# A modulation sum copied a step later, two more steps before transposing o, and a last tail of four slots

## The chip, the cores and the metric

The kernel runs on one core of a Trainium2 chip. The metric is device time in microseconds, the median of the runs of one program. All times inside the kernel are from one profiled execution and are counted from the start of its span.

## What is computed

Two transformer blocks on a sequence of 256 tokens of width 1024, in float32. The first has a SwiGLU feed-forward, a mixing layer of retention and neighbourhood attention, and a second SwiGLU. The second block has two layers, each an attention (the first blockwise, the second differential) and a squared-ReLU feed-forward, both followed by a layer norm with a gated residual. Shift, scale and gate of each come from sums over a second input `c`:

```python
mod = jnp.einsum('bd,lde->lbe', jax.nn.silu(c), ada_w) + ada_b[:, None, :]
for i in range(DEPTH_2):
    shift1, scale1, gate1, shift2, scale2, gate2 = [m[:, None, :] for m in jnp.split(mod[i], 6, axis=-1)]
    h = x * (1.0 + scale1) + shift1
    y = moba_attention(h, ...) if i % N_MIXERS == 0 else diff_attention(h, ...)
    x = layer_norm(DEEPNORM_ALPHA * x + (1.0 + gate1) * y, ln_g[i, 0], ln_b[i, 0])
    h = x * (1.0 + scale2) + shift2
    y = sq_relu_mlp(h, mlp_w_up[i], mlp_w_down[i])
    x = layer_norm(DEEPNORM_ALPHA * x + (1.0 + gate2) * y, ln_g[i, 1], ln_b[i, 1])
```

In the differential attention, with 8 heads of 128 columns:

```python
p = jax.nn.softmax(s, axis=-1)
w = (p[:, :, 0] - lam * p[:, :, 1]).astype(v.dtype)
o = jnp.einsum('bhqk,bhke->bhqe', w, v)
o = rms_norm(o, subln_g) * (1.0 - lambda_init)      # then @ w_out
```

## The kernel before

**Weights.** All weights stream through a ring. A slot is 1 MB of weights and has two halves, called pieces, of 128 x 1024 each. `load` (L70) brings a piece into one of 6 raw buffers, on SP's queue. `piece` (L103) makes two parts of it: ScalarE copies it, rounded, to `wh` (L115), and VectorE subtracts that from the raw one to make `wl` (L93), one piece behind (`flush`). A ring of 8 pieces holds them. Each product is three matmuls (L201): high by high, low by high, high by low. A half slot is 12 matmuls of 512 columns or 24 of 256, about 2.7 us.

**Steps.** The kernel is one sequence of instructions, written out in the order in which it is issued, and each engine takes its own in that order. After every half slot `tick` (L430) runs: `st.tick` issues up to two pieces ahead, or one piece of a modulation sum, and then `bg` (L415) advances every generator in `gens` by one step. A `yield n` in a generator waits n steps. `start(gen, wait)` (L424) lets a generator begin `wait` steps after the `bg` that comes next. What is issued in a step stands, on each engine, behind all that was issued before it and ahead of the matmuls of the next half slot. An instruction that waits holds up its engine.

**Modulation sums.** Twelve sums, one for each of six vectors in two layers. Each has 8 pieces of `ada_w`; VectorE adds each, multiplied by a column of silu(c), to `adacc` (L339). After the last, `ada_parts` (L346) splits the sum into three bfloat16 parts, one instruction a step: ScalarE's copy (L349), a subtraction (L351), a second copy (L353), a second subtraction (L355). The first piece of the next sum drains what is left (`ada_drain`, L403). A finished sum waits in `ada_out`, and `spare` (L373), called when a hidden tile has been made, issues 24 small matmuls that reduce it over the partitions (or, for a gate, spread it).

**Second attention** (`attention(1, ...)`, L1219). Slots: 2 for v of heads 0 to 3, then q and k of each two heads, then v of heads 4 to 7, then the output projection. `pair(j, q, k)` (L1234) is the generator of head j: scores and row maxima, a step, exponentials, a step, VectorE combines the two softmaxes (L1271), one or two steps, transposition of the scores and ScalarE's copy T (L1280, L1281), a step, the product with v (tile `ao`, L1302), ScalarE's squares (L1312), POOL's power, a step, VectorE scales o (L1318), and, for heads below `ONE[1][1]`, a step; then TensorE transposes o (L1322), and ScalarE and VectorE make the high and low parts of Y (L1328, L1329), which the output projection reads. `down` (L510) multiplies a slot into four PSUM banks, half by half. `down_tail` (L520) does the last two slots bank by bank, so that a bank's post-processing (`post.bank`) begins while the next bank is multiplied.

**Last feed-forward** (`mlp`, L750). For j from 2 to 15, `proj` multiplies up-slot j and starts `hidden(j)` (ScalarE's ReLU L778, VectorE's product L779, a step, high and low parts L546, L547), and `down` follows three tiles behind. After the loop come `down` of tile 13, then `down_tail` of tiles 14 and 15. Four tiles are kept. The last post-processing (`Last`, L672) makes for each bank a product with the gate, the residual, statistics (L650 to L652), and, for two banks that share rows, the mean and variance, POOL's power, four passes of normalisation (L681, L683) and the stores (L684).

Of the kernel before, what the change touches and what calls it, by code (L numbers as in the profile page):

```python
# [37 lines left out]
       ((2, 0), (1, 0), (1, 1), (1, 2), (1, 3), (0, 2), (0, 3)))  # L38
LOOK = 3.0
WAITS = ((0, 1, 0, 1, 0, 1, 0, 1), (0, 1, 0, 1, 0, 1, 0, 1))  # L40
ONE = ((7, 8), (8, 6))
RET_WAITS = (1, 3, 1, 3)
NA_WAITS = (3, 2, 5, 4)

# [127 lines left out]
def block_kernel(ctx, tc, A, out):  # L172
# [157 lines left out]
    def ada(key, h, w):  # L330
        l, s, i = key
        kb = 2 * i + h
        if kb == 0:
            ada_drain()
            adacc[0] = big.tile([128, D], F32, name="adacc")
            V.tensor_scalar(adacc[0], w, csil[:, 0:1], None, op0=OP.mult)
            return
        t = adacc[0]
        V.scalar_tensor_tensor(t, w, csil[:, kb:kb + 1], t, op0=OP.mult, op1=OP.add)  # L339
        if kb == 7:  # L340
            ada_now.append(ada_parts(l, s, t))
            start(ada_now[0])

    ada_now, ada_done = [], {}

# [14 lines left out]
    ada_out, adap, grows = [], [], {}  # L360
# [50 lines left out]
    def nxt():  # L411
        wi_[0] += 1
        return wi_[0] - 1
# [10 lines left out]
    def start(gen, wait=0):  # L424
        gens.append([gen, wait + 1])
# [15 lines left out]
    def mmA(o, wh, wl, x, s, e):  # L441

        mm(o, x[:, 0], wh, s, False)
        mm(o, x[:, 0], wl, False, False)
        mm(o, x[:, 1], wh, False, e)

    TS = (slice(0, 128), slice(128, 256))
# [62 lines left out]
    def down(accs, H, first):  # L510
        n = nxt()
        for kk, (wh, wl) in enumerate(st.use(n, D)):
            for t in range(2):
                for f in range(2):
                    fs = slice(512 * f, 512 * f + 512)
                    mmA(accs[t][f], wh[:, 0, fs], wl[:, 0, fs], H[:, kk, :, TS[t]], first and kk == 0, False)
            st.release(n, kk)
            tick()

    def down_tail(accs, hs, post, mid):  # L520

        ns = [nxt(), nxt()]
        w = [st.use(n, D) for n in ns]
        for t in range(2):
            for f in range(2):
                fs = slice(512 * f, 512 * f + 512)
                for i in range(2):
                    for kk in range(2):
                        wh, wl = w[i][kk]
                        mmA(accs[t][f], wh[:, 0, fs], wl[:, 0, fs], hs[i][:, kk, :, TS[t]], False, i == 1 and kk == 1)  # L530
                    if t and f and i == 0:
                        mid()
                if t and f:
                    for n in ns:
                        for h in range(2):
                            st.release(n, h)
                if t and f:
                    post.bank(t, f, st.ahead)
                    st.flush(post.low)
                else:  # L540
                    post.bank(t, f)
                    tick()
# [205 lines left out]
        down_tail(accs, [hid.pop(n - 2), hid.pop(n - 1)], p, mid)  # L748

    @with_exitstack  # L750
    def mlp(cx, turn, after, post, mid):
        hp = cx.enter_context(tc.tile_pool(name="hid", bufs=1))
        n = DFF2 // 256
        hid = {}
        accs = None

        def tile_of(j):
            hid[j] = hp.tile([128, 2, 2, S], F32R, name="H", bufs=4)
            return hid[j][:, :, 0], hid[j][:, :, 1]

        def hidden01(ps):
            q = [w2("q"), w2("q")]
            for t in range(2):
                SC.activation(q[t], ps[t], AF.Relu)
                V.tensor_tensor(q[t], q[t], ps[t], OP.mult)
            yield 1
            for j in range(2):
                for c in range(2):
                    for t in range(2):
                        PE.transpose(two(ps[j])[:, c, TS[t]], q[t][:, (2 * j + c) * 128:(2 * j + c + 1) * 128], ident)  # L770
                split(*tile_of(j), two(ps[j]))
            if ada_out:
                yield 1
                yield from spare(ps[0])

        def hidden(j, p):
            q = w2("q")
            SC.activation(q, p, AF.Relu)  # L778
            V.tensor_tensor(q, q, p, OP.mult)  # L779
            yield 1  # L780
            split(*tile_of(j), two(q))
            yield from spare(p)

        ps = [gu("u"), gu("u")]
        projT(ps, turn, lambda: start_now(hidden01(ps)))
        after()
        for j in range(2, n):
            b = gu("u")
            proj(b, lambda: start_now(hidden(j, b)))
            if j >= 3:  # L790
                if accs is None:
                    accs = [[acc("acc") for _ in range(2)] for _ in range(2)]
                down(accs, hid.pop(j - 3), j == 3)
        down(accs, hid.pop(n - 3), False)
        while n - 1 not in hid:
            bg()
        mid[0]()
        p = post(accs)
        down_tail(accs, [hid.pop(n - 2), hid.pop(n - 1)], p, lambda: mid[1](p))
        return p  # L800

    lam = const.tile([128, 2], F32, name="lam")
# [384 lines left out]
    mid, first = ffn_block(G_F2PRE)  # L1187
# [31 lines left out]
    def attention(l, turn, after, mid):  # L1219
        with tc.tile_pool(name=f"att{l}", bufs=1) as mp:  # L1220
# [13 lines left out]
            def pair(j, q, k):  # L1234
# [7 lines left out]
                hs = [slice(0, 64), slice(64, 128)]  # L1242
# [34 lines left out]
                for a in range(nh):  # L1277
                    p = acc("at")
# [6 lines left out]
                if tail:  # L1285
                    yield from room(1)
                    p = acc("ao")
                    live[0] += 1
                    late = 1
                else:  # L1290
                    p = gu("ao")
# [25 lines left out]
                    for c in range(2):  # L1317
                        V.tensor_scalar(two(o)[:, c], two(p)[:, c, 0:128], r[:, c:c + 1], None, op0=OP.mult)  # L1318
                if j < ONE[l][1]:
                    yield 1  # L1320
                for c in range(2):
                    PE.transpose(two(p)[:, c, 128:256], two(o)[:, c], ident)  # L1322
                yh, yl, p = two(YH[:, j]), two(YL[:, j]), two(p)[:, :, 128:256]
# [15 lines left out]
            vdone, tail = set(), []  # L1339
# [34 lines left out]
            accs = [[gu("oacc") for _ in range(2)] for _ in range(2)]  # L1374
# [4 lines left out]
            post = PostLn(accs, grows.pop((l, 2)))  # L1379
# [21 lines left out]
    def after_ln(l, i):  # L1401

        ac = []

        def prep():
            g, b = ln_cols(l, i)
            ln, s = (l, 3) if i == 0 else (l + 1, 0)
            ac.extend(ln_mod(f"m{l}{i}", g, b, plus1(f"s{l}{i}", modc(ln, s + 1)), modc(ln, s)))

        def mid(post):  # L1410
            turns[0] = turn_of(post.v, *ac, gu if i else acc)
            turns[0](0)
        return prep, mid

    post = None
    for l in range(2):
        last, ln = post, ln_rows(0, 1) if l else None
        post = attention(l, only1(turns[0]), (lambda: start(last.residual(ln), 1)) if l else nothing, after_ln(l, 0))
        with ada_pool():
            last, ln = post, ln_rows(l, 0)  # L1420
            post = mlp(only1(turns[0]), lambda: start(last.residual(ln), 1),
                       (lambda accs: Last(accs, grows.pop((1, 5)), ln_rows(1, 1))) if l else
                       lambda accs: PostLn(accs, grows.pop((0, 5))), (nothing, nothing) if l else after_ln(0, 1))


_SHAPES = {"x": (256, 1024), "ffn1_w_in": (1024, 5632), "ffn1_w_out": (2816, 1024), "w_mix_in": (1024, 6656),
# [61 lines left out]
```

## Time and profile before

| | us |
|---|---|
| median of 3 runs | 1298.73 (1296.03 to 1302.18) |
| the profiled execution | 1299.73 |
| its span, first to last instruction | 1297.8 |
| TensorE busy | 1244.4 |
| VectorE busy | 930.2 |
| ScalarE busy | 644.9 |
| mean granted clock of TensorE | 0.982 |

PE is TensorE, PEld its weight loads, DVE VectorE, ACT ScalarE, SP the engine that issues loads. The granted clock is a share of 2.4 GHz. A matmul's row shows when it began and a modelled end, so a stream of matmuls is best read by their starts.

### The profile page before, as it was taken

To read this page: it belongs to the slowest core of one execution; us is meant where nothing else is said; L and a number is where in the kernel's file an instruction comes from. 1 tells how busy PE (TensorE), PEld (TensorE's weight loads), DVE (VectorE), ACT (ScalarE), POOL (GpSimd) and SP (SyncE) were. 2 spreads that over 40 slices of the span, in tenths; PEclk is the share of its full clock that TensorE was granted. 3 is DMA by queue.
4 is the path that set the end of the run, shared out by engine and by line. 5 is a ranking of instruction groups with operands and counts; after the bars stand their busy time and mean duration, and the time that the engine had idled before them with its cause. 6 is when DMAs were issued, how large, how long until landed. Compare 5 with 4: busy or idle time off the path is not lost. (4 is left out here: it accounts for less than half of the span.)

```text
span 1297.8 us, 18953 instructions
## 1 busy us (share of the span) xinstructions
PE 1244.4 (96%) x7216; PEld 1071.9 (83%) x7222; DVE 930.2 (72%) x1292; ACT 644.9 (50%) x1040; POOL 37.9 (3%) x45
## 2 busy tenths in 40 slices
PE   8999989999999999999999999999989889999996
PEld 7888767888988878888889978999968877799995
DVE  5687757888677676868478657777877966775655
ACT  6453445655555465354456545544544455544440
POOL 0000000220000000000000000000000001000000
PEclk9999989999999999999999999999998999999998
DMA  8778676766556477988454346788865434576650
GB/s 299 265 257 288 220 254 176 249 206 199 211 186 224 158 236 239 313 277 285 157 179 134 110 130 197 250 282 277 273 208 168 131 98 146 168 246 220 225 195 33
DMA packets 167883, 271.67 MB, mean 209 GB/s; under 512 B 15888, under 2 KB 119664, under 8 KB 167792
## 3 DMA queue, kind: packets, MB, share of 16 engines
q1 hardware_dynamic: 161328, 268.36, 63.0%
q10 hardware_dynamic: 6464, 2.10, 0.7%
q8 instruction: 57, 0.93, 0.3%
q14 instruction: 34, 0.28, 0.1%
HBM read 269.37 MB, written 1.05 MB: 208 GB/s over the span
## 5 line engine op out<-in xcount | busy, mean ns | idle before, releaser
L93 DVE TENSOR_TENSOR wl<-raw,wh 128x1024 fp32r<-128x1024 f32 x392 | 467.8, 1220 | 48.9 <-ACT wh L115 48.1
L115 ACT ACTIVATE wh<-raw 128x1024 fp32r<-128x1024 f32 x392 | 398.0, 1054 | 143.1 <-issue 21.5
L201 PE MATMUL acc<-wh,H 128*128 128x512 f32 x864 | 283.4, 396 | 3.0 <-ACT wh L115 3.0
L201 PE MATMUL g<-wh,XX 128*128 128x512 f32 x832 | 268.5, 398 | 3.6 <-ACT wh L115 1.9
L201 PEld LDWEIGHTS acc<-wh,H 128*128 128x128 f32 x864 | 163.7, 189 | 37.7 <-ACT wh L115 3.9
L201 PEld LDWEIGHTS g<-wh,XX 128*128 128x128 f32 x832 | 159.0, 191 | 38.8 <-ACT wh L115 2.3
L201 PE MATMUL acc<-wl,H 128*128 128x512 f32 x432 | 170.1, 394 | 1.5 <-DVE wl L93 1.5
L201 PE MATMUL g<-wl,XX 128*128 128x512 f32 x416 | 164.3, 395 | 0.8 <-DVE wl L93 0.8
L201 PE MATMUL u<-XX,wh 128*128 128x256 f32 x896 | 162.4, 283 | 0.0
L201 PEld LDWEIGHTS u<-XX,wh 128*128 128x128 f32 x896 | 141.4, 192 | 2.0
L201 PE MATMUL u<-XX,wl 128*128 128x256 f32 x448 | 126.8, 283 | 0.0
L339 DVE SCALAR_TENSOR_TENSOR adacc<-raw,csil,adacc 128x1024 f32<-128x1024 f32 x84 | 107.4, 1279 | 0.8
L201 PEld LDWEIGHTS acc<-wl,H 128*128 128x128 f32 x432 | 82.0, 190 | 17.6 <-DVE wl L93 2.1
L201 PEld LDWEIGHTS g<-wl,XX 128*128 128x128 f32 x416 | 79.6, 191 | 17.3 <-DVE wl L93 1.1
L201 PEld LDWEIGHTS u<-XX,wl 128*128 128x128 f32 x448 | 85.9, 192 | 0.0
L778 ACT ACTIVATE q<-u 128x512 f32<-128x512 f32 x28 | 16.7, 598 | 118.5 <-PE u L201 118.5
L779 DVE TENSOR_TENSOR q<-q,u 128x512 f32<-128x512 f32 x28 | 19.2, 686 | 73.9 <-ACT q L778 73.9
L715 ACT ACTIVATE a<-g,r 128x256 f32<-128x256 f32 x44 | 20.5, 473 | 90.1 <-PE g L201 90.0
L717 DVE SCALAR_TENSOR_TENSOR b<-g,r,a 128x256 f32<-128x256 f32 x44 | 20.6, 481 | 55.7 <-ACT a L715 55.6
L201 PE MATMUL v<-wh,XX 128*128 128x256 f32 (+1 forms) x192 | 49.8, 346 | 5.9 <-DVE XX L608 5.4
L201 PE MATMUL k<-XX,wh 128*128 128x256 f32 x256 | 47.3, 286 | 0.0
L201 PE MATMUL q<-XX,wh 128*128 128x256 f32 x256 | 47.3, 286 | 0.0
(291 smaller groups left out, 1762.6 us busy)
## 6 DMA issues: line engine op xcount, KB each, us to landing
raw<-in_ada_w_dram SPq DMA_DIRECT2D x96, 512.0 KB, 5.1
raw<-in_ffn_w_in_dram SPq DMA_DIRECT2D x176, 256.0 KB, 4.8
raw<-in_mlp_w_up_dram SPq DMA_DIRECT2D x64, 512.0 KB, 4.4
raw<-in_mlp_w_down_dram SPq DMA_DIRECT2D x64, 512.0 KB, 4.9
raw<-in_w_mix_in_dram SPq DMA_DIRECT2D x52, 512.0 KB, 4.7
raw<-in_ffn_w_out_dram SPq DMA_DIRECT2D x44, 512.0 KB, 5.2
raw<-in_moba_w_in_dram SPq DMA_DIRECT2D x24, 512.0 KB, 4.5
raw<-in_diff_w_in_dram SPq DMA_DIRECT2D x24, 512.0 KB, 4.4
```

What stands on the lines that cost most here:

```text
L93: self.nc.vector.tensor_tensor(wl, raw, wh.bitcast(F32), OP.subtract)
L115: nc.scalar.activation(wh, raw, AF.Copy)
L201: PE.matmul(o, l, r, start=start, stop=stop, skip_group_check=True)
L339: V.scalar_tensor_tensor(t, w, csil[:, kb:kb + 1], t, op0=OP.mult, op1=OP.add)
L715: SC.activation(two(a)[:, t], ps[t][:, 0:256], AF.Silu, scale=r[0][:, t:t + 1])
L717: V.scalar_tensor_tensor(two(b)[:, t], ps[t][:, 256:512], r[0][:, t:t + 1], two(a)[:, t], op0=OP.mult, op1=OP.mult)
L778: SC.activation(q, p, AF.Relu)
L779: V.tensor_tensor(q, q, p, OP.mult)
```

## The change

Three places. A modulation sum's first copy begins one step later (`start(ada_now[0], 1)`). In the second attention every head now has at least one step between o and its transposition, and heads 0 to 3 have two. And in the last feed-forward `down_tail` takes four hidden tiles and four slots instead of two: it runs over as many as it is given, and `mlp` leaves the last `tail` tiles to it. The first feed-forward of the second block passes 2 and is as before.

```diff
-ONE = ((7, 8), (8, 6))
+ONE = ((7, 8), (8, 8))
...
-            start(ada_now[0])
+            start(ada_now[0], 1)
...
-        ns = [nxt(), nxt()]
+        ns = [nxt() for _ in hs]
         w = [st.use(n, D) for n in ns]
         for t in range(2):
             for f in range(2):
                 fs = slice(512 * f, 512 * f + 512)
-                for i in range(2):
+                for i in range(len(hs)):
                     for kk in range(2):
                         wh, wl = w[i][kk]
-                        mmA(accs[t][f], wh[:, 0, fs], wl[:, 0, fs], hs[i][:, kk, :, TS[t]], False, i == 1 and kk == 1)
-                    if t and f and i == 0:
+                        mmA(accs[t][f], wh[:, 0, fs], wl[:, 0, fs], hs[i][:, kk, :, TS[t]], False,
+                            i == len(hs) - 1 and kk == 1)
+                    if t and f and i == len(hs) - 2:
                         mid()
...
-                down(accs, hid.pop(j - 3), j == 3)
-        down(accs, hid.pop(n - 3), False)
+                if j - 3 < n - tail:
+                    down(accs, hid.pop(j - 3), j == 3)
+        if tail == 2:
+            down(accs, hid.pop(n - 3), False)
...
-        down_tail(accs, [hid.pop(n - 2), hid.pop(n - 1)], p, lambda: mid[1](p))
+        down_tail(accs, [hid.pop(i) for i in range(n - tail, n)], p, lambda: mid[1](p))
...
                 if j < ONE[l][1]:
-                    yield 1
+                    yield 1 + (l == 1 and j < 4)
...
-                       lambda accs: PostLn(accs, grows.pop((0, 5))), (nothing, nothing) if l else after_ln(0, 1))
+                       lambda accs: PostLn(accs, grows.pop((0, 5))), (nothing, nothing) if l else after_ln(0, 1), 4 if l else 2)
```

## Rows read from the trace of the kernel before

**Rows 1.** The page's first part: busy us (share of the span) x instructions.

```profile
PE 1244.4 (96%) x7216; PEld 1071.9 (83%) x7222; DVE 930.2 (72%) x1292; ACT 644.9 (50%) x1040; POOL 37.9 (3%) x45
```

**Rows 2.** Waits of TensorE: line, what was waited for, total us, times, longest.

```profile
PE ao L1322 <- DVE o L1318: 6.2, 4, 1.9
...
PE g L201 <- DVE ada L355: 0.7, 1, 0.7
```

**Rows 3.** Waits of ScalarE, same columns.

```profile
ACT ada L349 <- DVE adacc L339: 44.6, 11, 6.0
```

**Rows 4.** Stretches: length, busy us and instructions by engine, granted clock, DMA.

```profile
181.50:185.00 3.50, 2.74 (x7) 2.15 (x7) 3.50 (x4) 3.50 (x5) 0.00 (x0) 0.53 0.59 177
185.00:188.50 3.50, 3.50 (x10) 2.65 (x9) 3.50 (x4) 3.13 (x4) 0.00 (x0) 0.50 0.87 315
1032.00:1035.50 3.50, 3.24 (x29) 2.74 (x30) 3.46 (x10) 1.80 (x3) 0.00 (x0) 1.00 0.54 154
1052.00:1055.50 3.50, 3.50 (x20) 2.52 (x20) 2.99 (x7) 0.96 (x2) 0.00 (x0) 0.52 0.40 147
1078.50:1082.00 3.50, 3.36 (x19) 2.96 (x20) 1.87 (x4) 2.23 (x6) 1.07 (x1) 1.00 0.60 168
```

**Rows 5.** Timeline near 180: start, us, instruction [idle before, releaser].

```profile
176.48 0.60 ACT L546 ACTIVATE H<-g 128x512 fp32r<-128x512 f32 x1 [5.07 <-PE g L723]
179.03 1.06 ACT L349 ACTIVATE ada<-adacc 128x1024 bf16<-128x1024 f32 x1 [1.95 <-DVE adacc L339]
...
177.72 1.28 DVE L339 SCALAR_TENSOR_TENSOR adacc<-raw,csil,adacc 128x1024 f32<-128x1024 f32 x1
...
181.09 0.50 PE L201 MATMUL g<-wh,XX 128*128 128x512 f32 x1 [1.87 <-ACT wh L115]
182.35 0.79 PE L201 MATMUL g<-wl,XX 128*128 128x512 f32 x1 [0.76 <-DVE wl L93]
```

**Rows 6.** Timeline where the third and the eighth sum are finished and used.

```profile
190.16 1.21 DVE L355 TENSOR_TENSOR ada<-adacc,ada 128x1024 bf16<-128x1024 f32 x1
...
197.17 4.62 DVE L93 TENSOR_TENSOR wl<-raw,wh 128x1024 fp32r<-128x1024 f32 x4
...
199.22 0.74 PE L201 MATMUL g<-small,ada 128*128 128x1 bf16 x24
...
611.17 3.48 DVE L93 TENSOR_TENSOR wl<-raw,wh 128x1024 fp32r<-128x1024 f32 x3
...
613.22 0.74 PE L201 MATMUL g<-small,ada 128*128 128x1 bf16 x24
```

**Rows 7.** Timeline of the second attention, TensorE and VectorE.

```profile
1032.26 0.44 PE L1322 MATMUL ao<-cst,o 128*128 128x128 f32 x2 [1.89 <-DVE o L1318]
...
1061.04 0.48 PE L201 MATMUL as<-k,q 64*128 64x128 f32 x2 [1.03 <-ACT T L1281]
...
1078.64 0.44 PE L1322 MATMUL ao<-cst,o 128*128 128x128 f32 x2 [1.49 <-DVE o L1318]
...
1083.42 0.44 PE L1322 MATMUL ao<-cst,o 128*128 128x128 f32 x2 [0.94 <-DVE o L1318]
...
1031.60 0.61 DVE L1318 TENSOR_SCALAR o<-ao,r 128x128 f32<-128x128 f32 x2
...
1037.19 0.01 DVE L1227 LOAD_MASK_SELECT sh<-q  x1 [1.01 <-PE q L201]
```

**Rows 8.** Timeline of the last tail, TensorE and VectorE.

```profile
1265.38 0.40 PE L201 MATMUL acc<-wh,H 128*128 128x512 f32 x1
...
1286.94 0.39 PE L201 MATMUL acc<-wh,H 128*128 128x512 f32 x1
...
1266.21 0.69 DVE L779 TENSOR_TENSOR q<-q,u 128x512 f32<-128x512 f32 x1 [5.39 <-ACT q L778]
...
1287.07 0.68 DVE L650 TENSOR_TENSOR v<-acc,grow 128x512 f32<-128x512 f32 x1
...
1289.12 0.67 DVE L650 TENSOR_TENSOR v<-acc,grow 128x512 f32<-128x512 f32 x1
```

More of the change, by code (lines that the diff above doesn't have):

```diff
@@ L750, in mlp @@
     @with_exitstack
-    def mlp(cx, turn, after, post, mid):
+    def mlp(cx, turn, after, post, mid, tail):
         hp = cx.enter_context(tc.tile_pool(name="hid", bufs=1))
```

## The prediction

> **What bounds the kernel now.** I read the engines' busy times first: TensorE is busy for 1244.4 of the 1297.8 us of the span [rows 1], so the time is TensorE's own work, plus its waits (53 us), plus what its low clock costs. Then I read what TensorE waited for, in total and by place [rows 2]: only waits that stand there can be won back by moving work. The largest line of them is the transposition of o in the second attention, 6.2 us in four waits on VectorE's o. Next come ScalarE's waits [rows 3]: the first copy of a modulation sum makes ScalarE wait 44.6 us in 11 places for the last accumulation on VectorE. ScalarE is idle half of the span, so this costs only where a weight copy that TensorE needs stands behind it. Last I read the granted clock by stretch [rows 4]: full speed is 1.00 (2.4 GHz), 0.50 is 1.2 GHz. After some waits of about 2 us TensorE runs for some 3.5 us at 0.50, which loses 1.7 us more; after others of the same length it keeps 1.00.
>
> **Part 1, the sums' first copy one step later.** A step is one half slot (12 matmuls, 2.7 us). The copy was issued in the step of the accumulation it reads; now it is issued one step later, behind that step's two weight copies. The second copy and the two subtractions move with it, except where the next sum's first piece drains them at once. Nothing is added. Of the twelve sums the trace shows one, the third, that holds up TensorE. Its copy starts at 179.03, when the accumulation started at 177.72 is done (ScalarE had been ready since 177.08); the weight copies follow at 180, and TensorE waits 1.87 us for the first and 0.76 for its low part [rows 5]. With the copy moved, both weight copies run from 177.1. The low part stays behind the accumulation on VectorE: 179.0 plus 1.16 (4.62 over four) [rows 6] is 180.2, where TensorE, free at 179.2 with one matmul to do, wants it at 179.3. So 0.9 us of the 2.63 stays: **1.7 won**. These waits were followed by 0.53 and 0.50 over 7 us [rows 4]; 7 times 0.485, less the half of the 0.76 us of waiting inside, is 3.0: **3.0 won** if 0.9 us of waiting leaves the clock alone, from 0 if it does not.
>
> The price is at the other end of the chain. The matmuls that turn a sum into the modulation are issued by the next hidden step that finds it finished, and for two sums, the third and the eighth, that step stays the same while the last subtraction (L355, 1.21 us) comes one step later, behind that step's low parts. Third: low parts start at 197.17 once b is there; two of them, then L355, end 3.5 us later at 200.7; TensorE reaches the first of these matmuls at 199.22 [rows 6], and the third matmul reads the last part: 1.4 us of new waiting. Eighth: two low parts from 611.17, then L355, end at 614.7, against 613.22: 1.4. That such a wait is paid by TensorE is seen once already, 0.7 us at the first sum [rows 2]. **2.8 lost**; bounds 0 (if the low parts run earlier) and 2.8 plus 1.7 of low clock for each, 6.2. The other ten keep a step or more between, or are drained in the step in which they are drained now; their modulation DMA on SP is issued in the same step. One sum alone keeps a loop of steps running in the mixing; it gets one empty step more, and VectorE and ScalarE have slack there: 0, bounds -0.5 and 0.5. Part 1 together: 1.7 + 3.0 - 2.8 = **1.9 won**, from 4.5 lost to 4.7 won.
>
> A rule of the Trainium skill speaks against counting the clock. In "TensorE: Matmul & The Clock Gate", section "Why this matters for your kernels", it asks that TensorE be kept from idling long between bursts, and the gap it warns of is longer than every wait in rows 5 and 7. By it neither 181 nor 1052 would have lost the clock, and the sum below would be smaller by the 3.0 here and the 1.7 of part 2. The trace does not agree: the clock stands at 0.53 and 0.52 behind waits of 1.9 us [rows 4]. It agrees in part elsewhere, since the equal wait at 1032 was followed by 1.00.
>
> **Part 2, the transposition of o in the second attention.** Heads 0 to 3 get two steps between o (VectorE) and its transposition instead of one; heads 6 and 7 get one instead of none. Heads 4, 5 are unchanged. The four waits [rows 2, 7] are: heads 1 and 3, 1.89 each (the second by subtraction from 6.2), head 6, 1.49, head 7, 0.94. Heads 0 and 2 do not wait.
> Heads 1, 3: o ends at 1032.2 because VectorE first does the key's rotation (four operations), a low part, and the Y of head 0. One step more is 2.7 us against 1.9 of lateness: the wait goes. What could be late next is VectorE, which has 1.01 us of idle time at 1037.19 [rows 7] against the 1.89 that TensorE gains: it falls 0.9 behind there. Those that read what it makes next (the scores read the rotation, head 3's product takes the PSUM buffer that head 1's Y gives back a step later than now) come a step of 2.7 or more after it, which leaves it some 1.8, an estimate. What is added: head 1's and head 3's Y copy (0.47) now stands on ScalarE ahead of the copy of the transposed scores, for which TensorE already waits 1.03 at 1061.04 [rows 7]: 0.5 lost once, at head 3; at head 1 it fits while TensorE does the product. Transpositions themselves change place only (0.1 net). Head 3's wait was followed by 0.52 over 3.5 us [rows 4]: 1.7 won with it.
> Heads 6, 7: with a step between, o (ready at 1078.6 and 1083.4) is 1.7 and 0.9 us ahead of its reader; head 7's Y is then made in the last step before the output projection's tail, whose first nine matmuls (2.0 us) do not read it, against 1.2 for its two operations (0.47 and 0.48, with what lies between). No step is added, since the loop already has one after head 7. 2.4 won.
> Part 2: 1.9 + 1.9 + 1.5 + 0.9 + 1.7 - 0.6 = **7.3 won**; bounds 2.4 (heads 1 and 3 wait elsewhere) and 7.9.
>
> **Part 3, the last tail over four slots.** The matmuls are the same 96, from 1265.38; only their order changes: each of the four banks is finished after 24 instead of all being touched first. TensorE's end is unmoved, but the post-processing of the first three banks is now done before it. Today the last bank ends at 1287.3 (the last matmul starts at 1286.94 and takes 0.39), and VectorE, behind with the first rows' normalisation and the third bank, starts on it at 1289.12, at its own 2 us a bank [rows 8]. With 5.5 us between banks it starts at 1287.4. **1.7 won**; the rest of the chain to the stores is the same. Against it: the first bank now needs all four hidden tiles and weight slots 4 to 5 us after 1265.38. VectorE does the product at 1266.21, then a low part, the hidden tile's low part (0.6, of the product's size) and two more low parts: 1266.82 + 3 times 1.16 + 0.6 = 1270.9; the 23rd matmul, at 0.227 each (95 between 1265.38 and 1286.94), wants the last at 1270.4: **0.5 lost**, bounds 0 and 1.2 (one more low part ahead). The row loads of the last normalisation go out on SP 11 us earlier, behind nothing but weight loads that are out. Part 3: **1.2 won**, bounds 0.5 and 1.7.
>
> **Sum.** 1.9 + 7.3 + 1.2 = 10.4 against the profiled execution's own 1299.73 (span 1297.8, 1.9 outside it): **1289.3**. That execution is 1.0 above the median of the three runs; I leave this in, as it may be part of what is won.
>
> **Rivals.**
> (a) The waits move. VectorE is nearly full in the attention's first part; if its lag after 1037 exceeds the 1.8 us found above, the scores or the products wait for it, and heads 1 and 3 return nothing (3.3 + 1.7 less). For it: VectorE is busy for 3.46 of the 3.5 us from 1032 [rows 4]. Against: its idle time at 1037 and beyond. 1294.3.
> (b) The clock returns nothing: the removed waits at 181 and 1050 were not what lowered it, or waits as long remain near them. Then 3.0 and 1.7 are not won: 1294.0. For it: equal waits before 1032 and 1078 left the clock at full. Against: in both places the low stretch begins within half a microsecond of the wait. The page named above comes to the same result.
> (c) The two new waits of 1.4 us bring the low clock, 1.7 each: 1292.7. For it: 1.9 at 1050 did. Against: 1.5 before 1078.64 did not [rows 7], nor 1.9 before 1032.26.
> (d) Slower. Whether a wait lowers the clock depends on where it lies in time, and everything behind 180 us lies elsewhere. If waits that now pass at full clock lose it, at 1.7 apiece, seven of them outweigh the 10.4 won; ten give 1306.3. The rows show waits of equal length going either way [rows 4, 7], but ten the wrong way at once is a lot.
> (e) A step does not do what it says: the parts are drained, or o's lateness is not what the transposition waits for. The rows name the releaser in each place, so little speaks for it. 1299.
>
> **How the numbers follow.** Forecast 0.70 (its own range 1286 to 1292), (a) 0.11, (b) 0.07, (c) 0.06, (d) 0.03, (e) 0.03. A measurement of this kernel tells some 0.5%, 6.5 us, from no change, so faster means under 1292.2: nearly all of the forecast and a little of (a) and (c), 0.71; slower is (d), 0.03; the rest 0.26. The range for 8 in 10 takes in (a) to (c), and reaches from 1285.5 (part 1 at its upper bound, and the median's 1.0) to 1296.
>
> **What would show it.** In the changed profile: no wait of the transposition of o on VectorE over 0.3 us; the wait for the weight copy at 181 gone and 0.9 on a low part in its place, with 1.00 behind it; two waits of 1.4 us on L355, near 194 and 610; the wait for the transposed scores' copy at head 3 grown to about 1.5; VectorE's work on the last bank beginning within 0.1 us of TensorE's end, and about 0.5 us of waiting near the 23rd matmul of the tail. Wrong would be waits on the rotation or on Y in the attention, a new low stretch behind the L355 waits, or a tail in which TensorE ends later by more than 1.2.

## The result, and the profile after

The changed kernel takes 1287.45 us (median of five runs, 1284.54 to 1289.42), the kernel before 1298.73 (five runs beside it, 1294.49 to 1302.18): a ratio of 0.9913, 95% interval 0.9896 to 0.9930, or 11.3 us less (9.1 to 13.5). The prediction was 1289.3, faster. The profiled execution of the changed kernel took 1289.42, its span is 1287.5 (before 1297.8), its mean granted clock 0.986 (before 0.982). In this kernel's listing lines stand one to three lower: L1322 is now L1325, L1281 is L1284, L723 is L724, L650 is L651. All times here are of one profiled execution for each kernel; "shift" is how much earlier the changed kernel's row is than the row of before.

The busy times, to be read against [rows 1], and TensorE's waits, against [rows 2] (line, what was waited for, total, times, longest):

```profile
PE 1241.3 (96%) x7222; PEld 1069.9 (83%) x7222; DVE 931.4 (72%) x1292; ACT 645.8 (50%) x1040; POOL 38.0 (3%) x45
...
PE g L201 <- DVE ada L355: 2.8, 3, 1.3
```

VectorE and ScalarE do the same work as before, and TensorE the same matmuls. The 10.3 us of the span have three parts: TensorE is busy for 3.1 us less, which is clock, as far as modelled ends tell; its idle time between matmuls is 5.4 less (42.9 before, 37.5 now); and what comes behind the end of its last matmul is 1.7 less (10.5 before, from 1287.33 to 1297.84; 8.8 now, from 1278.75 to 1287.53). The line of the transposition of o, 6.2 us before, is gone from the list. The line on the last subtraction has grown from 0.7 to 2.8.

Near the third and the eighth sum, TensorE and VectorE (start, us, instruction, in brackets idle before and releaser):

```profile
178.55 0.50 PE L201 MATMUL g<-wl,XX 128*128 128x512 f32 x1 [0.77 <-DVE wl L93]
...
192.75 1.22 DVE L355 TENSOR_TENSOR ada<-adacc,ada 128x1024 bf16<-128x1024 f32 x1
...
192.53 0.19 PE L201 MATMUL g<-small,ada 128*128 128x1 bf16 x2
194.03 0.70 PE L201 MATMUL g<-small,ada 128*128 128x1 bf16 x22 [1.30 <-DVE ada L355]
...
608.13 1.22 DVE L355 TENSOR_TENSOR ada<-adacc,ada 128x1024 bf16<-128x1024 f32 x1
...
607.91 0.19 PE L201 MATMUL g<-small,ada 128*128 128x1 bf16 x2
609.40 0.70 PE L201 MATMUL g<-small,ada 128*128 128x1 bf16 x22 [1.30 <-DVE ada L355]
```

[Rows 5] showed waits of 1.87 and 0.76 in front of the projection; only 0.77, on the low part, is left. At both sums TensorE issues two of the 24 small matmuls and then waits 1.30 us for the third part, as VectorE makes it behind a low part.

Granted clock of the changed kernel in stretches behind waits (length, busy us and instructions by engine, granted clock, DMA; compare [rows 4]):

```profile
170.00:173.50 3.50, 3.50 (x8) 2.80 (x9) 2.28 (x2) 0.00 (x0) 0.00 (x0) 0.51 0.64 188
179.00:182.50 3.50, 3.50 (x17) 2.85 (x16) 3.50 (x4) 3.08 (x4) 0.00 (x0) 1.00 0.88 331
194.00:197.50 3.50, 3.47 (x35) 3.00 (x36) 3.50 (x4) 1.27 (x2) 0.00 (x0) 1.00 0.98 317
610.00:613.50 3.50, 3.50 (x14) 2.79 (x11) 2.29 (x4) 0.00 (x0) 0.00 (x0) 0.55 0.87 269
654.00:657.50 3.50, 3.50 (x11) 2.71 (x11) 3.10 (x4) 1.06 (x1) 0.00 (x0) 0.60 0.94 291
1054.00:1057.50 3.50, 3.50 (x19) 3.50 (x19) 3.15 (x8) 0.50 (x1) 0.00 (x0) 0.51 0.04 15
```

Full behind 179, where it was 0.53, and full behind the new wait at 194. Half behind the equally long new wait at 609.4, and half behind 1052.

The second attention ([rows 7]) and the last tail ([rows 8]):

```profile
1031.23 0.38 PE L1325 MATMUL ao<-cst,o 128*128 128x128 f32 x2
1044.05 0.38 PE L1325 MATMUL ao<-cst,o 128*128 128x128 f32 x2
1048.71 0.38 PE L1325 MATMUL ao<-cst,o 128*128 128x128 f32 x2
1052.00 0.48 PE L201 MATMUL as<-k,q 64*128 64x128 f32 x2 [1.40 <-ACT T L1284]
...
1041.38 0.01 DVE L1230 LOAD_MASK_SELECT sh<-k  x1 [0.53 <-PE k L201]
```

```profile
1256.11 0.40 PE L201 MATMUL acc<-wh,H 128*128 128x512 f32 x1
1261.69 0.50 PE L201 MATMUL acc<-wl,H 128*128 128x512 f32 x1 [0.17 <-DVE wl L93]
...
1278.36 0.39 PE L201 MATMUL acc<-wh,H 128*128 128x512 f32 x1
...
1278.79 0.69 DVE L651 TENSOR_TENSOR v<-acc,grow 128x512 f32<-128x512 f32 x1 [3.29 <-PE acc L201]
```

The transpositions of o stand without a bracket: no wait. VectorE's idle time near them has shrunk to 0.53, and the wait for the transposed scores' copy has grown from 1.03 to 1.40. In the tail the last matmul starts 22.25 us after the first (21.56 before), and VectorE starts on the last bank 0.04 us after the modelled end of that matmul (before, 1.79 after it).

**Where the 10.3 us of the span came from.** Transpositions that both kernels have serve as milestones. Before:

```profile
12.54 0.60 PE L865 MATMUL xt<-cst,X 128*128 128x128 f32 x4
...
630.24 0.60 PE L723 MATMUL g<-cst,b 128*128 128x128 f32 x4
...
970.30 1.09 PE L590 MATMUL xt<-cst,v 128*128 128x128 f32 x8 [1.01 <-ACT v L662]
...
1096.38 1.09 PE L590 MATMUL xt<-cst,v 128*128 128x128 f32 x8 [0.26 <-ACT v L662]
```

and after:

```profile
11.30 0.60 PE L868 MATMUL xt<-cst,X 128*128 128x128 f32 x4
...
627.99 0.60 PE L724 MATMUL g<-cst,b 128*128 128x128 f32 x4
...
968.20 1.09 PE L591 MATMUL xt<-cst,v 128*128 128x128 f32 x8 [1.01 <-ACT v L663]
...
1086.12 1.09 PE L591 MATMUL xt<-cst,v 128*128 128x128 f32 x8 [0.26 <-ACT v L663]
```

| stretch | shift at its end | won in it | forecast |
|---|---|---|---|
| start, up to the transposition of x at 12.54, now 11.30 | 1.24 | 1.2 | - |
| first sum (TensorE's wait 0.68, now 0.17) | 1.76 | 0.5 | 0 |
| third sum, up to its small matmuls (199.22, now 192.53) | 6.69 | 4.9 | 4.7 |
| the wait of 1.30 at 194, up to the eighth sum (613.22, now 607.91) | 5.31 | -1.4 | -1.4 |
| eighth sum: wait of 1.30, low stretch of 1.7 | 2.25 | -3.1 | -1.4 |
| 628 to 968 | 2.10 | -0.1 | 0 |
| behind 972 one low stretch, before two | 3.4 | 1.3 | - |
| second attention | 10.26 | 6.8 | 7.3 |
| behind 1099 two low stretches, before one, up to the tail | 9.27 | -1.0 | - |
| last tail | 10.33 | 1.1 | 1.2 |

Three lines of the table (start, 972, 1099) are low stretches at waits that no edit touches; they sum to 1.5.

### The profile page after: what moved, and what is told of

It reads as the page before. It is cut to its first block, busy times and chain, and to the rows that moved or that the text cites. A ratio compares the mean times of both kernels' runs of the same rounds, so it can differ in the third digit from the quotient of the medians.

```text
span 1287.5 us, 18963 instructions
## 1 busy us (share of the span) xinstructions
PE 1241.3 (96%) x7222; PEld 1069.9 (83%) x7222; DVE 931.4 (72%) x1292; ACT 645.8 (50%) x1040; POOL 38.0 (3%) x45
## 3 DMA queue, kind: packets, MB, share of 16 engines
HBM read 269.37 MB, written 1.05 MB: 210 GB/s over the span
## 4 chain that ended last, share of the span: by engine, by line
PE 83%; DVE 8%; ACT 4%; issue 2%; DMA 2%; POOL 1%; SPq 0%; DVEq 0%; ACTq 0%; POOLq 0%
PE acc L201 21%; PE g L201 20%; PE u L201 14%; DVE wl L93 4%; PE q L201 3%; PE k L201 3%; PE v L201 3%; PE oacc L201 3%; PE yr L201 2%; PE as L201 2%; PE rg L201 1%; PE ao L201 1%; ACT hf L604 1%; PE nq L201 1%; PE nk L201 1%
## 5 line engine op out<-in xcount | busy, mean ns | idle before, releaser
L115 ACT ACTIVATE wh<-raw 128x1024 fp32r<-128x1024 f32 x392 | 399.5, 1054 | 165.0 <-issue 26.5
L201 PE MATMUL g<-wh,XX 128*128 128x512 f32 x832 | 264.3, 392 | 1.7 <-DVE XX L598 1.7
L201 PEld LDWEIGHTS g<-wh,XX 128*128 128x128 f32 x832 | 156.2, 188 | 35.5 <-DVE XX L598 2.1
```

The lines of the kernel that those rows point to most:

```text
L115: nc.scalar.activation(wh, raw, AF.Copy)
L201: PE.matmul(o, l, r, start=start, stop=stop, skip_group_check=True)
```

## The experiments

Those with an interval are given as a ratio to the kernel before, run beside them on the same chip. Times won follow the ratio, and not the difference of two medians.

**One part at a time.** Three kernels are the kernel before with one part each: `start(ada_now[0], 1)`; the two edits of the second attention; `down_tail` over four slots.

> Part 1 alone on the kernel before. By the theory that a removed or added wait costs its length plus 1.7 us where the clock falls to half behind it: the two weight-copy waits at the third sum (1.87 and 0.76) shrink to one of about 0.8 and the two low stretches behind them go (4.7 won), two waits of 1.3 on the last subtraction come, near 194 and 610 (2.6 lost), and one low stretch behind the second of them, as in the changed kernel (1.7 lost): 0.4 won, about 1298.3. The prediction's own figure is 1.9 won, 1296.8. By the rival that the place of the low stretches is settled by place in time, some other stretches change sides and the result lies anywhere from 5 won to 5 lost with the same list of waits.

> Part 2 alone on the kernel before. By the theory: the four waits of the transposition of o are gone, the wait for the transposed scores' copy at head 3 is about 1.4, some 6.8 to 7.3 us won, about 1291.5 to 1292; nothing changes ahead of 1020 us. By the rival that the attention's waits only move when part 1 has not come first (VectorE's lag), waits on the scores, the rotation or Y stand there instead and 2.4 us are won, about 1296.

> Part 3 alone on the kernel before. By the theory VectorE starts on the last bank as TensorE ends (1.75 won) and TensorE's tail is 0.7 longer because the first bank wants the low parts of all four slots: 1.1 won, about 1297.6, and nothing is different ahead of 1255 us. By the rival that the tail is bounded by the last bank's own chain to the stores and TensorE's loss is paid in full: 0.7 lost.

| | median us | ratio, 95% | us won | forecast |
|---|---|---|---|---|
| part 1 | 1296.64 | 0.9986, 0.9971 to 1.0002 | 1.8 (-0.3 to 3.8) | 1.9 |
| part 2 | 1289.75 | 0.9942, 0.9920 to 0.9964 | 7.5 (4.7 to 10.4) | 7.3 |
| part 3 | 1296.48 | 0.9992, 0.9979 to 1.0005 | 1.0 (-0.6 to 2.7) | 1.2 |
| all three | 1287.45 | 0.9913, 0.9896 to 0.9930 | 11.3 (9.1 to 13.5) | 10.4 |

The parts add up (10.3 of 11.3), as far as intervals this wide can tell; only part 2's interval leaves out no change, and part 1's holds the 0.4 of its expectation as well as the prediction's 1.9. Part 2's waits do not move when part 1 is missing: no wait on o, 1.40 for the scores' copy, and no wait on the rotation beyond 0.2. Part 3's kernel shows the same tail as the full change: the last matmul 0.7 late, the last bank begun as TensorE ends.

In the clock these profiles differ at waits that the edits do not touch, as the rival of the first expectation had it. With part 1 alone the low stretches behind 130, 168 and 454 are missing, and new ones stand near 1028 and 1059. With part 2 alone the same three are missing and one of the two behind 181; one stands near 220, none stands behind the wait of 1.40, and the wait near 959 is 2.20 where it was 0.92. So the expectation that nothing changes ahead of 1020 did not hold.

**The sum handed on one step later.** The two waits of 1.30 come because the small matmuls go out in the very step in which the last subtraction is issued.

```diff
         V.tensor_tensor(parts[2], t, parts[1], OP.subtract)
-        yield 1
+        yield 2
         ada_now.clear()
         ada_out.append(...)
```

> The changed kernel with a finished sum handed on one step later, so that the third sum's small matmuls go out at the end of the feed-forward and the eighth's at the next hidden tile that comes after it. By the theory that the two waits on the last subtraction (1.30 each) are paid by TensorE in full and that the low stretch at 610 is the second one's: 4.3 won on the changed kernel, about 1283, full clock near 610 and no wait on the last subtraction but the first sum's 0.2. By the rival that the waits are covered by what comes after them (TensorE only arrives earlier at the next wait): 0 to 1 won, and the waits at 216, 218 and at the next hidden tiles grow by 1.3 each. By the rival that low stretches belong to places in time, one appears elsewhere and 2.6 are won.

Ratio 0.9893 (0.9870 to 0.9917), 1284.26 us: 3.2 below the changed kernel's median, span 4.4 shorter (1.3 of it at the first load, which no edit touches). The line on the last subtraction is gone from TensorE's waits, and with it the low stretch behind 609:

```profile
604.00:607.50 3.50, 3.50 (x19) 2.85 (x19) 3.50 (x4) 1.68 (x3) 0.00 (x0) 1.00 0.62 180
```

(1.00 where it was 0.55.) The third sum's small matmuls now stand where TensorE waited 0.64 for the mixing's activations; that wait is gone too. A low stretch came back behind 451 and a second one behind 773, which the edit does not touch. Behind the third sum the shift to the changed kernel grows by 1.9, the 1.30 and the 0.64; behind the eighth by 3.1, the 1.30 and 1.7 of clock. So the waits were paid in full, and the low stretch near 610 belonged to one of them; rival (c) of the prediction was half right.

**The same kernels once more.** Nothing is edited.

> The changed kernel once more, unaltered, for a second profiled execution. The waits should stand at the same places with the same lengths to 0.1 us. By the theory that the program settles where the clock falls to half, the low stretches stand at the same nine places. By the rival that this differs from one execution to the next (the runs of one kernel lie up to 7.7 us apart, some four stretches at 1.7 each), some of them are missing and others come, behind the same waits, and the span differs by 1.7 for each.

> The kernel before once more, unaltered, for a second profiled execution of it. The waits stand where they stood, to 0.1 us in length. Where the low stretches stand it is to show which of them belong to the kernel (the two behind 181, the one behind 1050) and which to the execution: by the reading of two executions of the changed kernel, those behind 130 and 168 may be missing, and those behind 181 and 1050 stay.

The second execution of the changed kernel has a span of 1284.0, 3.5 shorter, and its waits are the same, in place and, but for the first load and one of 0.64, to 0.05 us. What differs is the clock behind two of them. The waits and the clock of that second execution:

```profile
166.84 0.50 PE L201 MATMUL acc<-wh,H 128*128 128x512 f32 x1 [1.51 <-ACT wh L115]
168.10 0.50 PE L201 MATMUL acc<-wl,H 128*128 128x512 f32 x1 [0.76 <-DVE wl L93]
...
168.50:172.00 3.50, 3.50 (x19) 2.92 (x18) 1.90 (x3) 0.66 (x2) 0.00 (x0) 1.00 0.79 229
```

The stretch at 170 in the fence further up had the same two waits in front of it (1.51 and 0.75) and 0.51. The second execution of the kernel before, span 1296.3 against 1297.8, lacks only the low stretch of the first 11 us, and keeps those behind 181 and 1050. Over the profiled executions of the kernels in this document the count by wait is:

| wait of TensorE | us | profiles that have it | low clock behind it |
|---|---|---|---|
| weight copies near 130 and 168 | 1.5 + 0.8 | 13 | 7 (both places together) |
| weight copy near 181 | 1.9 + 0.8 | 4 | 4 |
| the same, low part alone | 0.8 | 8 | 0 |
| last subtraction near 194 | 1.3 | 6 | 0 |
| last subtraction near 609 | 1.3 | 6 | 6 |
| activations near 454 | 1.7 | 11 | 5 |
| second half's activations near 653, 780, 972, 1099 | 2.3 to 2.9 | 11 each | 10, 11, 11, 11 |
| o of head 1 | 1.9 | 5 | 2 |
| o of head 3 | 1.9 | 5 | 5 |
| scores' copy at head 3, part 2 in | 1.4 | 8 | 5 |

(At head 3, one of the five is the kernel with small matmuls, further down, which wait there themselves.) Each low stretch is some 3.5 us at 0.5 and costs 1.7, less what TensorE idles in it and what a later wait takes up. Behind the waits of 2.3 to 2.9 us in the table one came 43 times in 44. That is no rule of length: full clock followed a wait of 2.20 near 959 in the kernel with part 2 alone, and one of 2.31 for the first load, near 8, in the lag experiment below. For the waits under 2 us in the table it depends on the place, and in some places on the execution. Of the three lines without an edit in the table above, the first is the execution's: a low stretch at 7 to 11 us, which the second execution of the kernel before lacks. The other two are the same in both executions of each kernel, though the waits there are the same in both kernels: behind 972 there are two stretches in the kernel before and one in the changed one, behind 1099 one and two. They do not belong to the waits, though. The kernels with part 2 or part 3 alone have two behind 972 like before, that with part 1 alone has one; the kernel before with small matmuls at 181 and head 3 has one behind 972 and two behind 1099; and the changed kernel with VectorE delayed near 1036 has one behind 1099. What makes the difference, other than that everything lies elsewhere in time, stays open. The Trainium skill, "TensorE: Matmul & The Clock Gate", section "Part 1: The HAM clock gate", says that the moment at which the clock changes differs between runs of one kernel. It says so of the first matmuls; the two executions of the changed kernel show it behind 130 and 168 us.

**TensorE kept busy in a wait.** Two kernels put matmuls of no use into a wait, so that what is waited for comes as late as ever and only the idleness goes. The first is the kernel before, with small matmuls in front of the projection at 181 and of the transposition of o of head 3:

```diff
             else:
+                if j == n - 1 and wi_[0] < 40:
+                    warm(ps[0], 24)
                 projA(ps, XX, then=lambda: start_now(hidden(j, ps)))
...
                 if j < ONE[l][1]:
                     yield 1
+                if l == 1 and j == 3:
+                    for _ in range(24):
+                        mm(p[:, 384:512], identb, identb, True, True)
```

> The kernel before, with 24 small matmuls of no use (128 columns, some 1.4 us) in front of the waiting matmul in two places: the projection that waits 1.87 us for a weight copy at 181, and the transposition of o of head 3, which waits 1.89 near 1050. It keeps the lateness of what is waited for and takes away TensorE's idleness, so it measures the prediction's two clock terms by themselves (3.0 near 181 and 1.7 behind 1050). By the theory that idleness brings the low clock: in both places less than 0.6 us of waiting on the same releaser, no low stretch behind it near 181 (3.4 saved) and none within 1 us of the transposition of head 3 (1.7 saved, unless the wait for the transposed scores' copy behind it, 1.03, brings one of its own): 3.4 to 5.1 won, 1293.5 to 1295 beside 1298.7. By the rival that the waits themselves, not the idleness, or chance alone, decide: 0.

```profile
174.20 0.60 PE L723 MATMUL g<-cst,b 128*128 128x128 f32 x4
177.42 1.51 PE L201 MATMUL g<-identb 128*128 128x128 bf16 x24
179.44 0.51 PE L201 MATMUL g<-wh,XX 128*128 128x512 f32 x1 [0.51 <-ACT wh L115]
180.70 0.50 PE L201 MATMUL g<-wl,XX 128*128 128x512 f32 x1 [0.76 <-DVE wl L93]
...
194.22 0.60 PE L723 MATMUL g<-cst,b 128*128 128x128 f32 x4
...
180.70:184.20 3.50, 3.50 (x15) 2.91 (x16) 3.50 (x4) 3.50 (x5) 0.00 (x0) 1.00 0.63 204
...
1046.72 2.36 PE L201 MATMUL ao<-identb 128*128 128x128 bf16 x24 [1.89 <-DVE o L1320]
```

and the same two transpositions in the second execution of the kernel before, without small matmuls:

```profile
174.22 0.60 PE L723 MATMUL g<-cst,b 128*128 128x128 f32 x4
...
197.14 0.60 PE L723 MATMUL g<-cst,b 128*128 128x128 f32 x4
```

Near 181 it did what it should: the weight copy and the low part come as late as before, TensorE idles 0.51 and 0.76, and the clock behind is 1.00 where four profiles of the same code have two low stretches or one. Between the two transpositions 2.9 us are won (174.20 against 174.22, 194.22 against 197.14): that is the clock term by itself, forecast at 3.0 in the prediction and at 3.4 in the expectation, which left out that TensorE idles 0.76 us within the low stretches. At head 3 it failed: the small matmuls write the tile that VectorE's o still reads, so they waited 1.89 themselves and then took another 2.2 on the path, at half clock. Of this 0.8 comes back behind them, as the low stretch lies over them and not over what follows. 2.9 less 1.3 (2.15 less 0.83) is 1.6; measured were 1.2, with an interval from 0.3 lost to 2.6 won (ratio 0.9991, 0.9980 to 1.0002), which holds 1.6 but also no change at all. So the time of the whole kernel shows nothing here, and what is shown at 181 rests on the profile. The 1.7 behind head 3 stays untested in this way.

The second, on the changed kernel:

```diff
             turn(t)
+            if t:
+                warm(banks[t], 32)
             for i in range(2):
```

> The changed kernel with 32 small matmuls of no use (128 columns each, into a bank that the projection overwrites) in front of the first projection matmul of the second token half, four times: where TensorE now waits 2.3 to 2.9 us for the second half's rounded activations near 653, 780, 972 and 1099, each time with one or two low stretches behind it. By the theory that TensorE's idle time lowers the clock behind it: the wait shrinks to under 1 us, no low stretch follows in these four places, 5 of them are saved, 8.5 us, about 1279. By the rival that the number of low stretches depends on other things than these waits: 0, about 1287.5; and if the small matmuls run at half clock and last longer than the wait, up to 1 us lost in each place, 1291.

Ratio 0.9860 (0.9843 to 0.9877), 1280.99 us: 6.5 below the changed kernel's median; the span is 7.6 shorter. The edit reaches six places, not the four named: the mixing's first projection and the second feed-forward's (1.39 and 1.67 of waiting, now 0.47 and none) go through the same function. In the four places:

```profile
648.39 1.95 PE L201 MATMUL v<-identb 128*128 128x128 bf16 x32
651.12 0.50 PE L201 MATMUL v<-wh,XX 128*128 128x512 f32 x1 [0.79 <-DVE XX L611]
...
651.50:655.00 3.50, 3.50 (x16) 2.62 (x15) 3.29 (x5) 2.12 (x3) 0.00 (x0) 1.00 0.86 283
777.50:781.00 3.50, 3.50 (x16) 2.92 (x16) 3.28 (x4) 2.43 (x3) 0.00 (x0) 1.00 0.99 298
1095.00:1098.50 3.50, 3.50 (x16) 2.89 (x17) 3.26 (x4) 2.44 (x4) 0.00 (x0) 1.00 0.93 290
...
965.37 1.95 PE L201 MATMUL v<-identb 128*128 128x128 bf16 x32 [1.16 <-ACT hf L606]
```

The wait of 2.56 near 653 is down to 0.79, the projection begins no earlier behind its transposition, and the clock is 1.00 where it was 0.60. No low stretch is left in any of the four. In shifts they give 1.6, 1.6, 1.3 and 2.5, together 7.0 of the 8.5 that were expected. The rest of the 7.6 lies in places that the edit does not reach: no low stretch behind 130 and 168 in this execution (3.1 won), one at the start (1.2 lost) and a second one near 1046 (1.3 lost).

**How far VectorE may fall behind.** Rival (a) lived on a margin that was only estimated.

```diff
-                    V.scalar_tensor_tensor(yl, p, g, yh.bitcast(F32), op0=OP.mult, op1=OP.subtract)
+                    for _ in range(7 if j == 1 else 1):
+                        V.scalar_tensor_tensor(yl, p, g, yh.bitcast(F32), op0=OP.mult, op1=OP.subtract)
```

> The changed kernel with the low part of Y of head 1 computed seven times instead of once, in both attentions: some 2.3 us more of VectorE work near 1036 us (six times 0.39), where VectorE has no idle time until 0.53 us at 1041.38. It measures from which lag on rival (a) of the prediction decides. By the prediction's estimate (readers 1.8 us behind what VectorE makes) TensorE waits for nothing new. By the changed kernel's trace, in which the key's rotation ends at 1044.0 and the scores read it at 1044.69, the margin is 0.7, and 2.3 less 0.53 less 0.7 is 1.1 us of waiting on the rotated k at the scores near 1044; o and the combined softmax stay in time.

```profile
1035.24 3.60 DVE L1333 SCALAR_TENSOR_TENSOR Y<-ao,sm,Y 128x256 fp32r<-128x256 f32 x7
...
1043.19 0.74 DVE L1230 STREAM_SHUFFLE sh<-k 128x512 f32<-128x512 f32 x1
...
1045.98 1.06 PE L201 MATMUL as<-k,q 64*128 64x128 f32 x8 [1.92 <-DVE k L1234]
```

The wait is on the rotation, as the second reading expected, but 1.92 and not 1.1. The expectation took 0.39 an operation, the distance to a next one of another kind; seven of them in a row take 3.60, so six more are 3.1. VectorE has no idle time left ahead of the rotation at 1043.19, where the changed kernel had 0.53. That leaves 3.1 less 1.92, about 1.2, that VectorE could take without anyone waiting: 0.53 of idle time and some 0.65 of margin at the rotation's reader.

**A tail of three slots.** `3 if l else 2` instead of 4.

> The changed kernel with a last tail over three slots instead of four. By the theory that the first bank of four slots wants a low part too early: TensorE's tail, counted from its first matmul of the last three slots, loses its 0.17 us wait and the slow spots near it, VectorE starts on the last bank within 0.1 us of TensorE's end, and the 0.7 us that part 3 lost come back. By the rival that those slow spots belong to the slots' order and not to their number: nothing comes back.

```profile
1252.89 0.40 PE L201 MATMUL acc<-wh,H 128*128 128x512 f32 x1
...
1274.45 0.39 PE L201 MATMUL acc<-wh,H 128*128 128x512 f32 x1
...
1274.88 0.69 DVE L651 TENSOR_TENSOR v<-acc,grow 128x512 f32<-128x512 f32 x1 [0.88 <-PE acc L201]
```

The last matmul starts 21.56 after the first of these, as before the change, and VectorE is on the last bank 0.04 after its modelled end. The 0.7 are back: the loss was the number of low parts that the first bank needs at once.

**All of it.** The changed kernel with the later hand-over, the small matmuls in the waits and the tail of three.

> The changed kernel with three edits: the finished sum handed on a step later (as measured before, 1284.3), the small matmuls in the four waits, and a last tail over three slots instead of four. By the theory that the clock falls behind idle time: 1284.3 less 8.5, and 0.4 for the tail (its first bank wants the low parts of three slots, so TensorE's 0.7 us in the tail go, while the banks still lie 4.1 us apart, more than VectorE's 2 us a bank): about 1275.5. By the rival that the small matmuls don't keep the clock: about 1284. By the rival that the tail of three begins late on the last bank: 0 to 1 lost there.

1275.09 us (1274.76 to 1276.17), ratio 0.9817 (0.9800 to 0.9833): 23.8 us below the kernel before and 12.4 below the changed one. Two low stretches are left between start and end, at 7 and at 959:

```profile
960.15 3.44 PE L201 MATMUL v<-identb 128*128 128x128 bf16 x32 [1.16 <-ACT hf L606]
```

There the small matmuls had to wait for their bank, 1.16 us on ScalarE, and ran at half clock themselves, 32 in 3.44 us. In the kernel with these alone they waited the same 1.16 in the same place (965.37 above), and took 1.95 at full clock: again the same wait, and the clock either way. That the time comes so near the 1275.5 is in part luck, as far as one profile tells: the small matmuls were counted at 8.5 and gave 7.0 above, and this profile has no low stretch behind 130, 168 and the wait of 1.40, which no edit of this kernel reaches.

## Why the prediction was right, point by point

**What bounds the kernel.** Right in the main, with one slip: the 53 us were called TensorE's waits. Of them 42.9 lie between its matmuls, and 10.5 behind its last one, where VectorE's post-processing and the stores bound the time. Of the 10.3 us won, 8.6 are TensorE's waiting and clock; 1.7 come from the stretch behind its end, by part 3, whose own working had this right.

**Part 1, the weight copy at 181.** Right in mechanism and size: 0.9 of waiting was to stay, 0.77 did; 4.7 were to be won, 4.9 were, 2.0 of them waiting (forecast 1.7) and 2.9 clock (3.0). That the clock comes back there no longer rests on one execution: low in four of four profiles with the wait, in none of eight without the 1.87, and in none when the same wait was filled. Rival (b) falls here. So does, for this place, the rule, as the prediction read it, of the Trainium skill, "TensorE: Matmul & The Clock Gate", section "Why this matters for your kernels": the gap was 1.87 us.

**Part 1, the two new waits.** The waits were forecast at 1.4 and are 1.30, in both places, for the reason given. What was wrong is the term's clock: the price was put at 2.8 without any, with 1.7 for each wait as a bound only, and it is 2.6 plus 1.7, since the second wait brings the low clock in six profiles of six. The argument against it was that a wait of 1.5 before 1078 and one of 1.9 before 1032 had passed at full clock. The counts show what that is worth: the first passes in all five profiles that have it, the second in three of five. Part 1 in the profile is 0.5 + 4.9 - 1.4 - 3.1 = 0.9, not 1.9; alone and over many executions it is 1.8, with an interval that holds both.

**Part 1, the first sum.** Forecast at nothing, won 0.5: of the 0.7 in [rows 2] 0.17 is left. The sums that are drained by the next one's first piece were taken as unchanged; VectorE's order ahead of this drain did change. Which instruction made the difference was not tried.

**Part 2.** (The title's two more steps are two places: each head moved has one step more.) The four waits went; none came on the rotation or on Y. The copy at head 3 costs 0.37 more (forecast 0.5). VectorE was to be 0.9 behind with 1.8 of margin, which leaves 0.9; the lag experiment found about 1.2. Rival (a) was set aside for the right reason, if narrowly. The clock term, 1.7, is the step that did not hold: the low stretch left the wait for o and, in five profiles of eight, stands behind the wait of 1.40 for the scores' copy instead. In shifts: 2.1 won up to head 1's place (forecast 1.9), 3.9 at head 3 with its clock (3.6; a wait of 0.47 on v's copy is 0.26 now), 0.4 lost at the copy, 1.5 lost to the new low stretch at 1054, 2.7 won at heads 6 and 7 (2.4): 6.8.

**Part 3.** 1.75 was to be won, and VectorE does start with TensorE's end. The loss was mis-sized: 0.69 instead of 0.5, since TensorE is slowed at two low parts (its rows at 1260.55 and 1261.69) and not only at the last. 1.1 instead of 1.2.

**The sum.** 10.4 forecast. The parts in the profile give 8.8 (0.9 + 6.8 + 1.1), and 1.5 came from low stretches at waits that no edit touches. So the predicted time is nearer to the result than its terms deserve: a missed low stretch at 610 was offset by one that the profiled execution of before happened to have at its start. The profiled execution of the changed kernel, 1289.42, is also the slowest of its five runs, and its second profiled execution took 1285.84: that the first lies 0.1 from the 1289.3 is luck. Rival (d), that what lies elsewhere in time may lose the clock, is real, but in single stretches and in both directions (1.3 won behind 972, 1.0 lost behind 1099), not ten at once.

**A cover that was not seen.** The low stretch of before at 461 costs nothing: its 1.7 are gone at the next hidden tile, where the changed kernel, at full clock, waits 1.05 for b and has the same shift (5.36 ahead of it, 5.35 behind).

```profile
466.70 0.94 PE L724 MATMUL g<-cst,b 128*128 128x128 f32 x4 [1.05 <-DVE b L718]
```

The stretch in the kernel before:

```profile
461.70:465.20 3.50, 3.50 (x10) 2.70 (x9) 0.80 (x4) 3.41 (x11) 0.00 (x0) 0.52 0.59 204
```

## What to carry to other kernels

When an instruction is moved a step later, follow its chain to the end: the last link met its reader in the same step, and one more step there was worth more than half of what the move had won at the front. Price each wait of TensorE twice, once for its length and once for the 1.7 us of clock that may follow it, and count that second price over several executions before it goes into a sum. Where a wait cannot be removed, small matmuls into a bank that is about to be overwritten left the clock at full in eight places of ten. They should find that bank free: at head 3 they waited for it themselves and put 2.2 us on the path.

## What the runs showed of the hardware

Two executions of one program, with the same waits to 0.05 us, kept the clock at 1.00 or fell to 0.51 behind the same wait of 1.51 and 0.75 us; such a fall costs up to 1.7 us, so that three of them are about as much as lies between the runs of the changed kernel (4.9 us), and one near 461 cost nothing. A wait of 1.30 us was followed by half clock in one place six times of six and in another never in six. Filled with small matmuls, waits of 2.3 to 2.9 us left the clock at full in seven of eight places. In the eighth the small matmuls themselves had waited 1.16 us, but in the other kernel the same wait of 1.16 was followed by full clock.
